# A two-layer hybrid decoder trunk: a new opening with the memory and x laid out features first

## The chip, the cores and the metric

The kernel runs on one core of a Trainium2 chip. The metric is the device time of one execution in microseconds (us), the median of several runs. The engines are TensorE (PE), VectorE (DVE), ScalarE (ACT), GpSimd (POOL) and SyncE (SP). SP and ACT issue the DMAs.

## The reference, cut to what matters

Two layers, each with 512 rows of 1024 features in x and 256 fixed memory tokens of 1024 features. Both x and the memory are normed over their features before a projection:

```python
def rmsnorm(x, g):
    return x * rsqrt(mean(x * x, axis=-1) + 1e-6) * g

def memory_read(q, mem_n, w_mem_kv):          # mem_n = rmsnorm(mem, mem_norm_g)
    k, v = split(mem_n @ w_mem_kv)            # 4 heads of 128 each
    p = softmax(q @ k.T * 128 ** -0.5)
    return p @ v

def hybrid_layer(x, mem, ...):
    proj = rmsnorm(x, pre_g) @ w_in           # 6664 columns, for four groups of heads
    y = concat(retention, ssd, stick_breaking, memory_read, each times its gate) @ w_out
    return x + rmsnorm(y, post_g)
```

The factor rsqrt(...) is a single number for each row of x or of the memory. It can be applied to a row before the projection, or to the row's results after it.

## The kernel before, in words

**Numbers in two parts.** Every operand of a product is split into a high part (fp32r, a cast on ACT) and a remainder (a subtraction on VectorE), and a product is made of three matmuls: high by high, high by low, low by high (`mm3`, `split`, `Pair`). "A product" below is one such matmul.

**Weights.** They come as blocks of 1 MB (128 x 2048), in the order in which they are used, on ACT's queue (`w_load`). Two such buffers exist (NRAW = 2), so that the load of block b+2 waits until both halves of block b have been split. Each half is a sub-block of 128x1024, split by ACT (`wh<-raw`) and VectorE (`wl<-raw,wh`) into one of five pairs of buffers (NSUB = 5, `w_prefetch`). Each layer's first two blocks hold the weights of the memory's keys, one sub-block for each head; the next two those of its values; then come those of x, beginning with the values of the stick-breaking heads (`sb_v`).

**Memory.** k0 to k3 are the keys of the four heads (`mem_k`, 24 products of 128x256 each, one sub-block); v0 and v1 are the values, two heads each (`mem_v`, two sub-blocks and 48 products each). Together they are 192 products. Keys and v go to TensorE's banks `pj`; four of these exist, and four `mx`.

**Norms.** `mem_norm` loads the memory with its rows on the partitions, squares and sums it on ACT, takes the power -0.5 on GpSimd, multiplies on VectorE by the deviation and the gain, transposes it on TensorE (`transposed`) and splits the result. x's four tiles of 128 rows (t = 0 to 3) go the same way in `prenorm`, into `hTh` and `hTl`. At the start the kernel does both, with the keys' products between x's tiles. For the second layer the memory is normed again, in the middle of the output projection (`out_proj`). x's tiles are normed at its end, as each row tile gets its post-norm (`post`), and the second layer's keys are made there too.

**Order.** Each engine takes its instructions from its own row, in order. In what order they stand there is decided by the framework's scheduler, which walks through the written program with times of its own. Buffers come from pools that go round; an instruction that needs a buffer waits for its last reader.

Of the kernel before, what the change touches and what calls it, by code (L numbers as in the profile page):

```python
# [15 lines left out]
DEPTH = 2  # L16
# [87 lines left out]
NPAR = 8 * 4 + 8 + 32 + 32 + 4 + 4 + 8  # L104
PO = dict(convw=0, convb=32, dtb=40, alog=72, dskip=104, ssdg=108, memg=112)


def pack_params(conv_w, conv_b, dt_bias, a_log, d_skip, ssd_norm_g, mem_norm_g):
    out = np.empty((P, DEPTH, NPAR), np.float32)
    for l in range(DEPTH):  # L110
        o = out[:, l]
        o[:, 0:32] = conv_w[l].reshape(4, 8, P).transpose(2, 1, 0).reshape(P, 32)
        o[:, 32:40] = conv_b[l].reshape(8, P).T
        o[:, 40:72] = np.repeat(dt_bias[l], 4)[None]
        o[:, 72:104] = np.repeat(a_log[l], 4)[None]
        o[:, 104:108] = np.repeat(d_skip[l], 64).reshape(4, P).T
        o[:, 108:112] = ssd_norm_g[l].reshape(4, P).T
        o[:, 112:120] = mem_norm_g[l].reshape(8, P).T
    return out

# [39 lines left out]
class Builder:  # L160
# [4 lines left out]
    def __init__(self, tc, pools, args, taps=None):  # L165
# [12 lines left out]
        self.nc.gpsimd.memset(self.eps4[:], EPS)  # L178

# [90 lines left out]
    def split(self, src, h, l, hf):  # L270
        self.nc.scalar.copy(h, src)  # L271
        self.nc.vector.tensor_sub(l, src, hf)  # L272
# [10 lines left out]
    def w_init(self):  # L283
        self.raw, self.sub = {}, {}
        self.nsubs = 2 * DEPTH * NBLK
        self.w_dma = self.w_off = self.w_split = self.w_cur = 0

    def w_prefetch(self):
        while self.w_split < min(self.nsubs, self.w_cur + self.NSUB):
# [5 lines left out]
            self.split(src, h, l, h.bitcast(F32))  # L295
            self.sub[k] = (h, l)
            self.w_split += 1
            if k % 2:
                del self.raw[k // 2]
                self.w_load(k // 2 + self.NRAW)  # L300

    def w_load(self, b):
        while self.w_dma <= min(b, DEPTH * NBLK - 1):
            n = block_width(self.w_dma)
            r = self.wp.tile([P, 2 * SUBD], F32, tag="raw", name=self.name("raw"), bufs=self.NRAW)
            src = self.a["wts"][self.w_off:self.w_off + P * n]
            self.nc.scalar.dma_start(r[:, :n], src.rearrange("(p n) -> p n", p=P))
# [21 lines left out]
    def proj_a(self, x=None, nt=NT, extra=0):  # L329
# [6 lines left out]
        banks = [self.mx() if t > 1 else self.pj() for t in range(nt // per)]  # L336
        for s in range(2):
# [8 lines left out]
            self.w_prefetch()  # L346
        return banks
# [43 lines left out]
    def load_rows(self, src, t):  # L391
        x = [self.buf(), self.buf()]
        for i in range(2):
            self.nc.sync.dma_start(x[i], src[P * t:P * t + P, 512 * i:512 * i + 512])
        return x

    def mem_norm(self, l):
        xs = [self.load_rows(self.a["mem"], t) for t in range(2)]
        gB = self.bcast_row(self.a["mem_norm_g"][l:l + 1])
        hns = [self.normed(x, gB) for x in xs]  # L400
        ps = [Pair(self) for _ in range(4)]

        for t in range(2):
            def out(k, b):
                for j in range(2):
                    p = ps[k // 2 + j]
                    s = slice(P * t, P * t + P)
                    self.split(v3(b[:, 256 * j:256 * j + 256], 2), v3(p.h, 2)[:, :, s], v3(p.l, 2)[:, :, s], v3(p.hf, 2)[:, :, s])
            self.transposed(hns[t], out)
# [5 lines left out]

    def mem_k(self, h):
        if h % 2 == 0:
            self.kT.append(Pair(self, 512, "y"))
        k, s = self.kT[h // 2], slice(N_MEM * (h % 2), N_MEM * (h % 2) + N_MEM)
        b = self.proj_b(self.mx_, N_MEM)  # L420
        self.split(b, k.h[:, s], k.l[:, s], k.hf[:, s])

    def mem_v(self):
        self.mv.append(self.pair(self.proj_a(self.mx_, 2)[0], "y"))
# [417 lines left out]
    def out_proj(self, l):  # L842
# [4 lines left out]
        for kc in range(16):  # L847
# [9 lines left out]
            if kc % 2:  # L857
                self.w_prefetch()
            if kc == 8 and not last:
                self.mem_norm(l + 1)  # L860
# [28 lines left out]
        if not last:  # L889
            for h in range(HEADS):  # L890
                self.mem_k(h)
# [26 lines left out]
    def build(self):  # L918
        nc = self.nc
        self.hTh, self.hTl = self.fixed(KC * SEQ, F32R, "hTh"), self.fixed(KC * SEQ, F32R, "hTl")  # L920
        self.hk = (lambda kc: self.hTh[:, SEQ * kc:SEQ * kc + SEQ], lambda kc: self.hTl[:, SEQ * kc:SEQ * kc + SEQ])
        self.w_init()
        nc.sync.dma_start(self.C[:, 0:P], self.a["consts"][:, 0:P])
        self.mem_norm(0)
        self.w_prefetch()
        preB = self.bcast_row(self.a["pre_norm_g"][0:1])
        self.xsrc = [self.a["x"][P * t:P * t + P] for t in range(NT)]
        for t in range(NT):
            self.prenorm(self.load_x(t), preB, t)
            self.mem_k(t)  # L930
        nc.sync.dma_start(self.C[:, P:NCON], self.a["consts"][:, P:NCON])
        nc.sync.dma_start(self.C[:, NCON:NCON + DEPTH * NPAR], self.a["params"])
        nc.vector.tensor_copy(self.b16[:, 0:P], self.con("ident", P))
        nc.vector.tensor_copy(self.b16[:, P:2 * P], self.con("neg", P))
        nc.vector.tensor_copy(self.onesr[:], self.con("ones", P))
# [4 lines left out]

    def layer(self, l):
        self.exp_ln_phase()
        for _ in range(2):
# [30 lines left out]
def lay_out(x, mem, pre_norm_g, post_norm_g, w_in, conv_w, conv_b, dt_bias, a_log, d_skip, ssd_norm_g, mem_norm_g,  # L974
# [3 lines left out]
        "mem": mem.reshape(N_MEM, D),  # L978
        "pre_norm_g": pre_norm_g,
        "post_norm_g": post_norm_g,  # L980
        "mem_norm_g": mem_norm_g,
        "wts": pack_weights(w_in, w_mem_kv, w_out),
        "params": pack_params(conv_w, conv_b, dt_bias, a_log, d_skip, ssd_norm_g, mem_norm_g).reshape(P, DEPTH * NPAR),
# [16 lines left out]
```

## Time and profile before

| | us |
|---|---|
| median of 3 runs | 982.67 |
| lowest and highest | 981.52, 983.36 |
| the profiled execution | 983.62 |
| its span from first to last instruction | 981.9 |
| TensorE busy | 956.9 |
| VectorE busy | 655.2 |
| ScalarE busy | 457.0 |
| GpSimd busy | 108.3 |

A row of the page or of a view has its time first, then its length, engine, line, operation, what it writes and reads (out<-in by the program's names), shapes and count; in brackets is how long the engine was idle before it and what ended that. All times are from the span's start. Products overlap in TensorE, so the distance between two starts is the price of one, not the length of its row. In a view of stretches each engine has its busy time and its count, in the order PE, PEld (weight loads), DVE, ACT, POOL, and then come the granted clock, the DMA engines' busy share and GB/s.

### The profile page before, as it was taken

How to read it: one execution, taken by the hardware profiler on the slowest of the kernel's cores; microseconds unless marked ns; L12 is line 12 of the kernel's file. 1: busy time of each engine (PE TensorE's matmuls, PEld its weight loads, DVE VectorE, ACT ScalarE, POOL GpSimd, SP SyncE). 2: the span in 40 equal slices, each digit the busy share in tenths (PEclk: the TensorE clock that was granted, in tenths of full speed). 3: DMA queues.
4: the chain of work that ended last, by engine and by line, in shares of the span. 5: the costliest groups of instructions: out<-in, count | busy, mean ns of one | idle time of the engine just before them, and what ended most of it. 6: DMA issues, size and time to landing. Idle time of an engine off the chain costs nothing.

```text
span 981.9 us, 13235 instructions
## 1 busy us (share of the span) xinstructions
PE 956.9 (97%) x5136; PEld 810.5 (83%) x5136; DVE 655.2 (67%) x1047; ACT 457.0 (47%) x848; POOL 108.3 (11%) x170
## 2 busy tenths in 40 slices
PE   3999999999999999999999999999999999999997
PEld 3998888988888788788899888898888878888885
DVE  5754566875867896766287455768776877867443
ACT  4733456633444443554265344765434543435341
POOL 1200000000242201020022000000002321102001
PEclk9999999999999999999999999999999999999999
DMA  9432211213142323264254321212123423323502
GB/s 356 156 130 86 84 46 44 86 49 123 44 144 102 119 91 126 74 204 155 102 195 151 130 86 44 86 44 86 49 84 93 140 97 118 113 91 119 191 24 85
DMA packets 26734, 106.84 MB, mean 109 GB/s; under 512 B 4144, under 2 KB 4528, under 8 KB 16944
## 3 DMA queue, kind: packets, MB, share of 16 engines
q10 hardware_dynamic: 10944, 79.76, 22.9%
q1 hardware_dynamic: 15728, 26.24, 8.3%
q8 instruction: 40, 0.66, 0.3%
q14 instruction: 22, 0.18, 0.1%
HBM read 101.68 MB, written 4.28 MB: 108 GB/s over the span
## 4 chain that ended last, share of the span: by engine, by line
PE 86%; DMA 5%; DVE 5%; ACT 1%; issue 1%; POOL 1%; DVEq 0%; SPq 0%; ACTq 0%; POOLq 0%
PE pj L263 63%; PE mx L263 20%; DMA s<-acs 1%; DMA r<-row 1%; DMA consts<-params 1%; DVE s L519 1%; PE mx L379 1%; DMA s<-mem 1%; DVE s L682 1%; PE mx L473 1%; DVE wl L272 1%; DMA t<-r 1%; POOL t L583 1%; DVE s L518 0%; DVE s L272 0%
## 5 line engine op out<-in xcount | busy, mean ns | idle before, releaser
L263 PE MATMUL pj<-hTh,wh 128*128 128x512 f32 x704 | 280.5, 398 | 0.0
L263 PE MATMUL pj<-hTl,wh 128*128 128x512 f32 x704 | 278.9, 396 | 0.0
L263 PE MATMUL pj<-hTh,wl 128*128 128x512 f32 x704 | 278.8, 396 | 0.0
L272 DVE TENSOR_TENSOR wl<-raw,wh 128x1024 fp32r<-128x1024 f32 (+1 forms) x152 | 185.7, 1224 | 126.2 <-ACT wh L271 119.8
L271 ACT CAST wh<-raw 128x1024 fp32r<-128x1024 f32 (+1 forms) x152 | 159.1, 1049 | 187.2 <-PE pj L263 155.6
L263 PEld LDWEIGHTS pj<-hTh,wl 128*128 128x128 f32 x704 | 132.3, 188 | 29.6 <-issue 0.2
L263 PEld LDWEIGHTS pj<-hTl,wh 128*128 128x128 f32 x704 | 132.4, 188 | 28.9
L263 PEld LDWEIGHTS pj<-hTh,wh 128*128 128x128 f32 x704 | 132.5, 188 | 28.3
L263 PE MATMUL pj<-wh,s 128*128 128x512 f32 (+1 forms) x384 | 105.0, 358 | 0.0
L263 PE MATMUL mx<-s,s 128*128 128x256 f32 (+4 forms) x616 | 97.6, 310 | 0.4 <-DVE s L272 0.4
L263 PEld LDWEIGHTS mx<-s,s 128*128 128x128 f32 (+1 forms) x616 | 84.5, 178 | 13.5 <-issue 3.2
L263 PE MATMUL mx<-wh,s 128*128 128x512 f32 x256 | 80.3, 393 | 0.0
L263 PEld LDWEIGHTS pj<-wh,s 128*128 128x128 f32 x384 | 68.0, 188 | 11.4
L263 PE MATMUL pj<-wl,s 128*128 128x512 f32 (+1 forms) x192 | 68.3, 356 | 0.0
L272 DVE TENSOR_TENSOR s<-mx,s 128x512 fp32r<-128x512 f32 (+2 forms) x100 | 47.1, 503 | 30.5 <-ACT s L271 30.3
L602 POOL TENSOR_SCALAR_AFFINE_SELECT s<-s 128x128 fp32r<-128x128 f32 x64 | 21.1, 362 | 417.6 <-DVE s L272 417.6
L263 PE MATMUL pj<-wh,hTh 128*128 128x256 f32 (+1 forms) x224 | 64.4, 287 | 0.4 <-DVE s L430 0.4
L271 ACT CAST s<-mx 128x512 fp32r<-128x512 f32 (+2 forms) x100 | 41.1, 446 | 49.2 <-PE mx L263 25.3
L263 PE MATMUL pj<-wl,hTh 128*128 128x256 f32 (+1 forms) x224 | 63.7, 284 | 0.0
L263 PE MATMUL pj<-wh,hTl 128*128 128x256 f32 (+1 forms) x224 | 62.9, 284 | 0.0
L263 PEld LDWEIGHTS mx<-wh,s 128*128 128x128 f32 x256 | 48.1, 188 | 10.9
L272 DVE TENSOR_TENSOR s<-y,s 128x512 fp32r<-128x512 f32 x64 | 41.3, 687 | 20.3 <-ACT s L271 14.5
(147 smaller groups left out, 1312.2 us busy)
## 6 DMA issues: line engine op xcount, KB each, us to landing
raw<-wts ACTq DMA_DIRECT2D x74, 1024.0 KB, 4.8
s<-x SPq DMA_DIRECT2D x24, 256.0 KB, 3.7
s<-acs SPq DMA_DIRECT2D x16, 256.0 KB, 6.6
r<-row SPq DMA_DIRECT2D x12, 256.0 KB, 3.7
raw<-wts ACTq DMA_DIRECT2D x2, 1056.0 KB, 5.2
s<-mem SPq DMA_DIRECT2D x8, 256.0 KB, 7.0
s<-acs SPq DMA_DIRECT2D x16, 128.0 KB, 5.5
x<-s SPq DMA_DIRECT2D x8, 256.0 KB, 2.3
```

Of the source, the lines that this page charges most:

```text
L263: return self.nc.tensor.matmul(out, lhsT, rhs, start=start, stop=stop)
L271: self.nc.scalar.copy(h, src)
L272: self.nc.vector.tensor_sub(l, src, hf)
L379: self.nc.tensor.transpose(b[:, P * j:P * j + P], hn[i][:, P * j:P * j + P], self.con("ident", P))
L473: nc.tensor.transpose(b[:, P * t:P * t + P], w[t // 2][:, o:o + P], self.con("ident", P))
L519: nc.vector.tensor_tensor_scan(out=u[:, ::-1], data0=u[:, ::-1], data1=u[:, ::-1], initial=0.0, op0=ALU.add, op1=ALU.bypass)
L583: nc.gpsimd.tensor_tensor(out=c, in0=c, in1=self.mhalf[:RP], op=ALU.pow)
L602: nc.gpsimd.affine_select(out=d, in_=d, pattern=[[1, P]], compare_op=ALU.is_ge, fill=0.0, base=0, channel_multiplier=-1)
L682: nc.vector.scalar_tensor_tensor(out=acc[:, s:], in0=b[:, :SEQ - s], scalar=tap(3 - s), in1=acc[:, s:], op0=ALU.mult, op1=ALU.add)
```

## The change

- **Layout.** The host passes x and the memory also with features on the partitions (`xT`, `memT`). Nothing is transposed on TensorE for the memory or for the first layer's x. Between the layers x is still normed and transposed as before.
- **Memory.** The raw memory times its gain is split (`mem_pairs`), and the keys and values are made of that. The deviation of each memory row comes from squares (ACT), additions (GpSimd), a product with a column of ones (`col_rstd`) and a power; `to_rows` spreads it as a row over all partitions by a product of ones with a diagonal matrix. Keys are multiplied by that row on VectorE before they are split (`mem_k2`), values by a column in their split (`mem_v`). The deviation is worked out once and used in both layers.
- **x of the first layer.** Its eight chunks of 128 features are squared, added up and normed in the same manner (`squares`, `col_rstd`, `to_rows`, `first_norm`); every second remainder is made on GpSimd.
- **Order.** The opening (`start`) is written by hand: its instructions enter their engines' rows in the order written. The scheduler takes over after it.
- **First work.** TensorE does 24 products of zeros (`warm_up`) while the first loads run. The first weight block is loaded and split in smaller pieces.
- The parameters get eight more columns (the gain of x's first norm).

The diff, cut to its core:

```diff
+    def warm_up(self):
+        self.nc.gpsimd.memset(self.b16[:], 0.0)
+        b = self.mx()
+        for _ in range(24):
+            self.mm(b[:, 0:2 * P], self.b16[:, 0:P], self.b16[:], True, True)
...
-    def proj_a(self, x=None, nt=NT, extra=0):
+    def proj_a(self, x=None, nt=NT, extra=0, mid=None):
...
             self.w_prefetch()
+            if s == 0 and callable(mid):
+                mid()
...
+    def mem_pairs(self, l, i):
+        nc, ps = self.nc, self.mp
+        for kc in (2 * i, 2 * i + 1):
+            p, s, g = ps[kc // 2], slice(256 * (kc % 2), 256 * (kc % 2) + 256), self.par(l, "memg", kc)
+            m = self.mraw[kc // 2][:, s]
+            nc.scalar.activation(p.h[:, s], m, AF.Copy, scale=g)
+            nc.vector.scalar_tensor_tensor(out=p.l[:, s], in0=m, scalar=g, in1=p.hf[:, s], op0=ALU.mult, op1=ALU.subtract)
+
+    def squares(self, raws, acc=None):
+        nc = self.nc
+        for x in raws:
+            q = self.buf()
+            nc.scalar.activation(q, x, AF.Square, scale=1.0 / 32.0)
+            if acc is None:
+                acc = q
+            else:
+                nc.gpsimd.tensor_tensor(out=acc, in0=acc, in1=q, op=ALU.add)
+        return acc
+
+    def col_rstd(self, sq, n, r):
+        b = self.mx()
+        for t in range(n):
+            self.mm(b[:, t:t + 1], sq[:, P * t:P * t + P], self.con("ones", 1), True, True)
+        self.nc.vector.tensor_scalar(out=r, in0=b[:, :n], scalar1=EPS, scalar2=None, op0=ALU.add)
+        self.nc.gpsimd.tensor_tensor(out=r, in0=r, in1=self.mhalf[:, :n], op=ALU.pow)
+
+    def to_rows(self, r, n):
+        d = self.buf(P * n)
+        for t in range(n):
+            self.nc.vector.tensor_scalar(out=d[:, P * t:P * t + P], in0=self.con("ident", P), scalar1=r[:, t:t + 1],
+                                         scalar2=None, op0=ALU.mult)
+        b = self.mx()[:, :P * n]
+        self.mm(b, self.con("ones", P), d, True, True)
+        return b
...
-        b = self.proj_b(self.mx_, N_MEM)
-        self.split(b, k.h[:, s], k.l[:, s], k.hf[:, s])
+        t = self.buf(N_MEM)
+        self.nc.vector.tensor_tensor(out=t, in0=b, in1=self.mrow[:], op=ALU.mult)
+        self.split(t, k.h[:, s], k.l[:, s], k.hf[:, s])
...
+    def first_norm(self, xs, rows, first):
+        H, HF, L = self.hTh[:], self.hTh[:].bitcast(F32), self.hTl[:]
+        for kc, x in enumerate(xs, first):
+            s = slice(SEQ * kc, SEQ * kc + SEQ)
+            self.nc.vector.scalar_tensor_tensor(out=x, in0=x, scalar=self.par(0, "preg", kc), in1=rows, op0=ALU.mult, op1=ALU.mult)
+            self.nc.scalar.copy(H[:, s], x)
+            (self.nc.gpsimd if kc % 2 else self.nc.vector).tensor_tensor(out=L[:, s], in0=x, in1=HF[:, s], op=ALU.subtract)
...
+            if kc == 6 and not last:
+                self.mem_load(nc.sync, range(4))
             if kc == 8 and not last:
-                self.mem_norm(l + 1)
+                self.mem_tiles()
+                for i in range(4):
+                    self.mem_pairs(l + 1, i)
...
             for h in range(HEADS):
-                self.mem_k(h)
+                self.mem_k2(h, self.mem_k(h))
...
+    def start(self):
+        nc = self.nc
+        self.warm_up()
+        nc.sync.dma_start(self.C[:, NCON:NCON + DEPTH * NPAR], self.a["params"])
+        self.mem_load(nc.sync, (0, 1))
+        self.w_load(1)
+        nc.sync.dma_start(self.C[:, 0:4 * P], self.a["consts"][:, 0:4 * P])
+        self.mem_tiles()
+        self.mem_pairs(0, 0)
+        self.w_prefetch(1)
+        for i in range(1, 4):
+            self.mem_pairs(0, i)
+        k = [self.mem_k(0)]
+        self.w_prefetch(2)
+        xT = [self.buf() for _ in range(KC)]
+        for kc in range(KC):
+            i = nc.sync.dma_start(xT[kc], self.a["xT"][:, SEQ * kc:SEQ * kc + SEQ])
...
+        q = self.squares([self.mraw[i] for i in range(2)])
+        k.append(self.mem_k(1))
+        self.w_prefetch(3)
+        q = self.squares([self.mraw[i] for i in range(2, 4)], q)
+        nc.gpsimd.tensor_tensor(out=q[:, :N_MEM], in0=q[:, :N_MEM], in1=q[:, N_MEM:], op=ALU.add)
+        self.w_prefetch(4)
+        k.append(self.mem_k(2))
+        self.col_rstd(q, 2, self.mcol[:])
+        k.append(self.mem_k(3))
+        self.w_prefetch(5)
+        q = self.squares(xT[:2])
+        nc.scalar.copy(self.mrow[:], self.to_rows(self.mcol, 2))
+        for h in range(2):
+            self.mem_k2(h, k[h])
+        self.w_prefetch(6)
+        q = self.squares(xT[2:5], q)
+        for h in range(2, HEADS):
+            self.mem_k2(h, k[h])
+        q = self.squares(xT[5:], q)
+        r = self.tiny(NT)
+        self.w_prefetch(7)
+        self.mem_v(lambda: self.col_rstd(q, NT, r))
+        self.w_prefetch(8)
+        rows = self.to_rows(r, NT)
+        self.first_norm(xT[:4], rows, 0)
+        self.w_prefetch(9)
+        self.mem_v(True)
+        self.first_norm(xT[4:], rows, 4)
```

98 lines of the change are left out of this document (53 added, 45 removed).

## The prediction

> **What bounds the kernel now.** I read the page first, then TensorE's waits, the chain that ended last, and counts of products by stretch.
>
> ```profile
> span 981.9 us, 13235 instructions
> PE 956.9 (97%) x5136; PEld 810.5 (83%) x5136; DVE 655.2 (67%) x1047; ACT 457.0 (47%) x848; POOL 108.3 (11%) x170
> PE   3999999999999999999999999999999999999997
> PE mx L379 <- DVE s L371: 15.1, 2, 14.9
> PE mx L263 <- DVE r L619: 1.8, 2, 0.9
> ```
>
> TensorE is busy for 97% of the span. Only the first slice is low, and of its waits one is long: 14.9 us for the first transposes; the next group has 1.8 in all. So the time is a start, then TensorE's own list of work. A change gains by starting that list earlier or shortening it, and loses wherever it makes TensorE wait.
>
> The chain of waits shows the start:
>
> ```profile
> 1.23 7.99 DMA s<-mem
> 9.24 9.46 DMA consts<-params
> 19.97 14.46 PE pj L263 x108
> 34.43 0.44 PE mx L379 x4
> ```
>
> The first product starts at 19.97 us; four transposes take 0.44, so one is 0.11. Next, TensorE's products in four stretches (after the range: length, then busy time and count; TensorE comes first):
>
> ```profile
> 19.97:23.70 3.73, 3.73 (x17) 3.73 (x18) 3.34 (x8) 3.14 (x8) 0.14 (x1) 1.00 1.05 402
> 23.70:27.43 3.73, 3.73 (x34) 3.73 (x33) 0.00 (x1) 0.00 (x0) 0.09 (x1) 1.00 0.66 248
> 511.50:524.50 13.00, 13.00 (x113) 13.00 (x113) 13.00 (x19) 9.98 (x20) 3.82 (x6) 1.00 0.50 166
> 14.94 1.97 PE L379 MATMUL mx<-consts,s 128*128 128x128 f32 x8 [14.94 <-DVE s L371]
> ```
>
> Between 511.5 and 524.5 us a 128x256 product takes 13.00/113 = 0.115. The first 3.73 us hold 17 products, the next 34: TensorE begins at half speed, though the granted clock reads 1.00 in both, and that costs 3.73/2 = about 1.9. The last row shows eight transposes in 1.97 after the idle start, also slow; they did not end the half speed.
>
> To compare starts I use one mark: the moment by which all 192 products of the memory and all of x's transposes would be done if TensorE did nothing else. Before, that is 19.97 + 192 x 0.115 (22.1) + 32 x 0.11 (3.5) + 1.9 = **47.4**. The changed kernel has no transposes of x; its mark is when TensorE can take x's first products.
>
> **The new start.** The prices, by group, busy us and mean ns:
>
> ```profile
> L272 DVE TENSOR_TENSOR wl<-raw,wh 128x1024 fp32r<-128x1024 f32 x12 | 14.5, 1222 | 11.6 <-ACT wh L271 11.6
> L271 ACT CAST wh<-raw 128x1024 fp32r<-128x1024 f32 x13 | 13.4, 1046 | 12.3 <-PE pj L263 4.7 <-DMA raw<-wts 4.7 <-PE mx L263 2.9
> L371 DVE SCALAR_TENSOR_TENSOR s<-s,t,s 128x512 f32<-128x512 f32 x12 | 8.5, 749 | 3.0 <-POOL t L357 3.0
> L366 ACT ACTIVATE s<-s 128x512 f32<-128x512 f32 x12 | 7.5, 627 | 1.5 <-DMA s<-mem 1.1 <-DMA s<-x 0.4
> L272 DVE TENSOR_TENSOR hTl<-mx,hTh 128x512 fp32r<-128x512 f32 x8 | 5.3, 684 | 0.0
> L272 DVE TENSOR_TENSOR y<-pj,y 128x256 fp32r<-128x256 f32 x4 | 1.6, 418 | 0.0
> L271 ACT CAST y<-pj 128x256 fp32r<-128x256 f32 x4 | 1.4, 372 | 0.0
> L934 DVE CAST b<-consts 128x128 bf16<-128x128 f32 x1 | 0.2, 220 | 0.0
> L729 POOL TENSOR_SCALAR_AFFINE_SELECT s<-s 128x512 f32<-128x512 f32 x16 | 13.8, 871 | 20.8 <-DVE s L728 18.5 <-ACT s L731 1.3 <-issue 1.0
> 6.12 1.99 ACT L271 CAST wh<-raw 128x1024 fp32r<-128x1024 f32 x2 [3.13 <-DMA raw<-wts]
> ```
>
> First product: the last row has the first 1 MB of weights in at 6.12. Now half of it suffices, beside params and a first part of the memory, so between 5 and 6.1. Two memory casts (2 x 0.37), a half cast and a half subtraction (about 0.55 and 0.65) follow: **7.6**, 12.4 earlier than before. The products on zeros run before it and cost nothing, as nothing else is there to do.
>
> From there k0 to k3 and v0's first half are 120 products, 13.8 us. The memory's column sums and its row product are small f32 products: between 0.12 and 0.45 each by the rows above, together 0.9. Feeding costs waits: ACT has by k3's weights 8 x 0.37 + 4 x 1.05 + 4 x 0.63 = 9.7 us to do from 5.5 on, then a subtraction of 1.22, so k3 can't start before 16.5; waits of 1 to 4 in all, I take 2.5. End of v0's first half: **24.8**.
>
> There TensorE needs the sum of x's squares (col_rstd stands in the middle of v0), and this is where the change loses. ACT's row, first before, then changed (y is k's pair, raw the next weight block, s_339 to s_362 x's squares):
>
> ```order
> 23 L366 ACTIVATE s46_197,t45_196<-s43_192 128x512
> 24 L271 CAST wh54_248<-raw33_172 128x1024
> 25 L271 CAST y51_221<-pj53_223 128x256
> 26 L366 ACTIVATE s47_198,t45_196<-s44_193 128x512
> 27 L271 CAST wh66_310<-raw38_182 128x1024
> 28 L271 CAST y51_221<-pj65_285 128x256
> ```
>
> Now six squares of x stand behind the DMA issue of block 4, which waits until VectorE has split block 2:
>
> ```order
> 24 L1041 COPY mrow_81<-mx52_322 128x256
> 25 L284 CAST y18_156<-s53_325 128x256
> 26 L284 CAST y18_156<-s54_329 128x256
> 27 L284 CAST wh55_333<-raw23_187 128x1024
> 28 L326 DMA raw57_337<-wts 128x2112
> 29 L441 ACTIVATE s58_339<-s26_191 128x512
> 30 L441 ACTIVATE s59_342<-s27_192 128x512
> 31 L441 ACTIVATE s60_345<-s28_193 128x512
> 32 L284 CAST y42_253<-s61_348 128x256
> 33 L284 CAST y42_253<-s62_352 128x256
> 34 L441 ACTIVATE s63_356<-s29_194 128x512
> ```
>
> Two more squares follow row 34. That a row waits for the one ahead is seen before:
>
> ```profile
> 28.17 1.05 ACT L271 CAST wh<-raw 128x1024 fp32r<-128x1024 f32 x1 [4.69 <-PE pj L263]
> 29.39 0.63 ACT L366 ACTIVATE s<-s 128x512 f32<-128x512 f32 x1
> 26.00:28.00 2.00, 2.00 (x20) 2.00 (x20) 0.00 (x0) 0.00 (x0) 0.00 (x0) 1.00 0.11 43
> ```
>
> ACT idled 4.69 us at the cast (row 24) though x, the last load of that phase, was in (DMA share 0.11 from 26 us), and squared only behind it.
>
> The walk: row product done at 22.0; mrow 22.5; VectorE multiplies by mrow (0.42), y cast, subtraction and next multiplication, y cast: 24.7; cast of weights 25.7; subtraction 27.0; DMA issue 27.4; three squares 29.3; two casts with their VectorE steps 31.0; three squares **32.9**. GpSimd adds each square to the sum. No row has a 128x512 addition of two inputs there; bounds are 0.87 (the one-input select) and twice that. I take 1.2, nearer to the row. The chain of adds then ends at **35.3**: TensorE is idle for 10.5. The Trainium skill, page "GPSIMD Engine Reference", section "3.1 Elementwise — side-by-side cycle accounting", gives 4497 ns for an addition of 2048 elements, by an estimate of a quarter 1.12; by it the sum would be 0.4 lower, and no row before tests it.
>
> After 10.5 idle I count half speed again, as after the idle start: four small sums and 24 products end at 40.3. Then v0's two scalings (0.74), cast, subtraction (stands ahead on VectorE), four diagonal multiplications at 0.22 and hand-overs: 44.5, so 4.0 idle. Row product 0.8, 48 products 5.5, and half speed again between 0 and 1.9, I take 1.0: 51.8. Meanwhile VectorE makes x's first four chunks (4 x 0.75 + 2 x 0.69, two waits for ACT): 50.9; only then stands the split of the next weights, 2.3, and a hand-over: mark **54.0**, or **+6.6**. Chunks 4 to 7 are hidden behind x's products with the first half of two weight blocks (96 products, 11 us).
>
> On the half speed: the rows show it after 15 us of idleness and never after under 1. The Trainium skill, page "TensorE: Matmul & The Clock Gate", Part 1, says the clock falls back after an idle window of about 3.4 us, which speaks against every new wait here; by it the 4.0 costs a full 1.9 and the sum is 0.9 higher.
>
> **The layer boundary.** The second memory pass loses 16 transposes, **-1.8**. But k now goes through a multiplication by mrow on VectorE before TensorE's bank comes free, and v0 needs the first of these banks. VectorE before, and the changed kernel's (y906 the second pair of k, L371 and L394 the normed t=2, L475 the multiplications by mrow):
>
> ```order
> 523 L272 TENSOR_TENSOR wl909_4842<-raw851_4530,wh908_4841 128x1024
> 524 L272 TENSOR_TENSOR y906_4815<-pj907_4816,y905_4814 128x256
> 525 L272 TENSOR_TENSOR y906_4815<-pj911_4849,y905_4814 128x256
> 526 L272 TENSOR_TENSOR wl913_4875<-raw901_4779,wh912_4874 128x1056
> 527 L272 TENSOR_TENSOR hTl_80<-mx874_4634,hTh_79 128x4x128
> 528 L905 TENSOR_TENSOR s886_4711<-mx799_4295,s785_4265 128x512
> 529 L371 SCALAR_TENSOR_TENSOR s881_4676<-s828_4412,t883_4681,s786_4268 128x512
> ```
>
> In the changed kernel the reads of the banks have moved from ahead of t=2 to behind it:
>
> ```order
> 514 L394 SCALAR_TENSOR_TENSOR s851_4611<-s798_4347,t853_4616,s756_4203 128x512
> 515 L394 SCALAR_TENSOR_TENSOR s852_4612<-s799_4348,t853_4616,s757_4204 128x512
> 516 L980 SCALAR_TENSOR_TENSOR s800_4351<-s761_4210,t858_4649,s800_4351 128x512
> 517 L980 SCALAR_TENSOR_TENSOR s801_4352<-s856_4646,t858_4649,s801_4352 128x512
> 518 L285 TENSOR_TENSOR hTl_80<-mx854_4621,hTh_79 128x4x128
> 519 L475 TENSOR_TENSOR s872_4716<-pj868_4685,mrow_81 128x256
> 520 L475 TENSOR_TENSOR s876_4749<-pj873_4720,mrow_81 128x256
> ```
>
> TensorE's row now, from the end of k3 on (pj884 k3, L402 transposes of t=1 and t=2, pj888 v0); before, v0 followed k3 at once and filled the time:
>
> ```order
> 2595 L276 MATMUL pj884_4790<-s726_4045,wl820_4462 128x256
> 2596 L402 MATMUL mx844_4569<-consts_72,s841_4559 128x128 x4
> 2597 L402 MATMUL mx845_4576<-consts_72,s842_4560 128x128 x4
> 2598 L402 MATMUL mx854_4621<-consts_72,s851_4611 128x128 x4
> 2599 L402 MATMUL mx855_4628<-consts_72,s852_4612 128x128 x4
> 2600 L276 MATMUL pj888_4824<-wh834_4532,s720_4039 128x256
> ```
>
> When that is, on before's clock:
>
> ```profile
> 511.33 0.28 PE L263 MATMUL pj<-s,wl 128*128 128x256 f32 x1
> 511.44 0.28 PE L263 MATMUL pj<-wh,s 128*128 128x256 f32 x1
> 514.76 0.75 DVE L272 TENSOR_TENSOR y<-pj,y 128x256 fp32r<-128x256 f32 x2
> 517.79 1.41 DVE L371 SCALAR_TENSOR_TENSOR s<-s,t,s 128x512 f32<-128x512 f32 x2
> ```
>
> k3 ends and v0 begins at 511.4. VectorE is full from 511.5 to 524.5 (13.00 above). Without the four y subtractions (1.4) t=2 is normed from 517.79 - 1.4 = 516.4 on. TensorE: t=1's transposes end at 512.3, t=2's halves run at 517.1 and 517.8; then VectorE's two of L980, hTl and the first L475 end at 520.1, so v0 starts at 520.2. Idle 520.2 - 511.4 - 1.8 of transposes = **7.0**, and half speed after it, 1.9 (transposes did not end it at the start): **+8.9**.
>
> The rest of the second pass I cost at nothing. SP issues the memory's four loads earlier, ahead of the last row of deviations:
>
> ```profile
> 419.37 1.00 SPq L394 DMA_DIRECT2D s<-mem  x2
> 423.79 0.33 SPq L587 DMA_DIRECT2D r<-row  x1
> 427.75 1.42 DVE L818 SCALAR_TENSOR_TENSOR y<-y,consts,r 128x512 f32<-128x512 f32 x2 [5.04 <-DMA r<-row]
> 453.33 2.77 DVE L866 TENSOR_TENSOR s<-pj,s 128x512 f32<-128x512 f32 x4 [1.17 <-PE pj L263]
> ```
>
> Four issues are some 2 us, so y comes at about 430 instead of 428; its products are the last of the half that ends at 453, some 20 us later. Without that cover each us late would count in full. The casts of the memory on ACT and VectorE take the place of its squares, normed rows and splits, behind the same products.
>
> Sum: 6.6 - 1.8 + 8.9 = 13.7. The profiled execution took 983.62; that gives 997.3. The median, 982.67, stands 0.95 under it: **996.4**. The rest of the list only shifts: TensorE's work there is the same.
>
> **Rivals.**
> - Boundary covered (VectorE reaches L475 by 512): 8.9 goes, 987.5. Against it: the fixed order and a full VectorE. 0.08.
> - x's sum ready by 25: 10.5, its half speed 1.9 and the 1.0 go, about 983; within 0.2% (2 us, about what a measurement tells). 0.04.
> - Faster: the waits do not hold the queues, that is, ACT and VectorE reach the later rows while the earlier wait. Both places vanish: mark 24.8 + 0.5 + 2.8 + 0.8 + 5.5 + 0.8 = 35.2, 12.2 under before's 47.4, with -1.8 is 968.7. It decides from x's sum being done by 25 and L475 by 512. The 4.69 row speaks against. 0.07.
> - GpSimd's adds dear. Under a busy VectorE a small operation took ten times its usual time:
>
> ```profile
> 522.97 2.28 POOL L351 TENSOR_SCALAR t<-t 128x1 f32<-128x1 f32 x1 [4.80 <-ACT s L366]
> 23.56 0.22 POOL L351 TENSOR_SCALAR t<-t 128x1 f32<-128x1 f32 x1 [7.32 <-ACT s L366]
> ```
>
> At 2.3 per add, six from 28.0 end at 41.8, 6.5 later: 1003. 0.08.
> - The zeros do nothing: k0 at half speed, +1.9, 998. Inside the forecast.
>
> Forecast 0.73. Faster 0.07, same 0.04, slower 0.89. The range leaves out the cases under 986 (0.11): 986 to 1003.
>
> **Right or wrong.** Right if TensorE's waits show one of 9 to 12 us at about 25 for GpSimd's sum, one near 40 for the diagonal, and 4 to 6 near the boundary for the normed t=2, then products of half rate. Wrong if first x-products start before 47, or if v0 of the second layer follows k3 within 2 us.

## The result and the profile after

| | before | after |
|---|---|---|
| median, us | 982.19 (4 runs) | 1010.01 (4 runs) |
| lowest and highest | 981.52, 983.36 | 1009.66, 1011.76 |
| the profiled execution | 983.62 | 1009.8 |
| its span | 981.9 | 1008.0 |

The ratio is 1.0285, with an interval of 1.0268 to 1.0303: 27.8 us slower, where 13.7 were forecast. Two executions, one of e6_scheduler below (3401.80 us) and one of the kernel before beside e12_paced_chunks (1056.26 us), lie far off all others and are left out of the times. The page of the changed kernel, its span, TensorE's busy time, and TensorE's rows of busy time and of granted clock in forty slices:

```profile
span 1008.0 us, 13162 instructions
PE 967.6 (96%) x5112; PEld 816.0 (81%) x5112; DVE 657.6 (65%) x1056; ACT 457.3 (45%) x834; POOL 116.7 (12%) x164
PE   7489999999999999999997999999999999999997
PEclk9689999999999999999998999999999999999999
```

The low first slice has become three (7, 4, 8), and a new one stands in the middle (a 7, at the layer boundary). The clock is below 1.00 in both places. TensorE's list of waits:

```profile
PE mx L276 <- POOL s L445: 12.2, 1, 12.2
PE mx L402 <- DVE s L394: 6.0, 1, 6.0
PE mx L276 <- DVE s L460: 5.3, 2, 4.7
PE pj L276 <- ACT wh L284: 2.3, 2, 2.0
```

The first three are the waits that the prediction named: GpSimd's sum of x's squares, the normed tile t=2 at the boundary, and the diagonal. To see how much each place took, two marks late in the program serve, which do the same work in both kernels: GpSimd's first masking of a stick-breaking head, and a reciprocal of the second layer. Before:

```profile
227.49 1.80 POOL L602 TENSOR_SCALAR_AFFINE_SELECT s<-s 128x128 fp32r<-128x128 f32 x7 [181.29 <-DVE s L272]
600.34 0.17 DVE L458 RECIPROCAL t<-t 128x2 f32<-128x2 f32 x1
```

After:

```profile
244.31 1.77 POOL L671 TENSOR_SCALAR_AFFINE_SELECT s<-s 128x128 fp32r<-128x128 f32 x7 [163.56 <-DVE s L285]
625.45 0.17 DVE L527 RECIPROCAL t<-t 128x2 f32<-128x2 f32 x1
```

The opening cost 244.31 - 227.49 = **16.8** (forecast 6.6), the boundary 625.45 - 600.34 - 16.8 = **8.3** (forecast 8.9 - 1.8 = 7.1). The last 1.0 of the span's 26.1 came later. So the boundary was sized well and the opening was not.

The opening by the chain of work that ended last (start, length, engine, what):

```profile
21.00 0.62 PE mx L276 x4
...
30.95 0.64 ACT s L441
...
39.53 1.27 POOL s L445
40.84 7.21 PE mx L276 x32
...
51.74 0.88 DVE s L460 x4
52.75 2.06 PE mx L276 x2
...
61.49 0.98 ACT wh L284
62.50 1.48 DVE wl L285
64.02 2.94 PE pj L276 x22
```

Read downwards it is the walk of the prediction: memory's sums (21.00), x's squares (30.95), GpSimd's additions to 40.8, x's column sums and 24 products, diagonal and row product, x's chunks, then the split of x's first weights. TensorE takes up x's products for good at 64.02, against the forecast mark of 54.0.

The granted clock in stretches of 3.4 us (range, length, busy time and count of each engine, then clock, DMA share, GB/s):

```profile
7.45:10.86 3.41, 3.41 (x14) 3.18 (x15) 3.41 (x8) 3.28 (x8) 0.00 (x0) 0.50 1.05 432
41.60:45.00 3.40, 3.40 (x17) 3.40 (x17) 0.16 (x1) 0.00 (x0) 1.04 (x1) 0.50 0.00 0
48.45:51.86 3.41, 0.00 (x0) 0.00 (x0) 2.23 (x4) 1.56 (x3) 0.00 (x0) 0.99 0.00 0
55.27:58.65 3.38, 3.38 (x18) 3.38 (x17) 2.32 (x4) 1.58 (x3) 0.30 (x1) 0.50 0.24 95
```

The clock was half for k0's first products, in spite of the zeros. It was half again from 31.3 us to 48.4, came back just as TensorE had run out of work, fell at 51.8 and was half until 58.65. All of TensorE's work between 40.8 and 58.6 ran at half rate.

At the boundary, by the timeline of each engine, TensorE's transposes and v0's first product, and VectorE's multiplications that free the bank:

```profile
526.77 1.04 PE L402 MATMUL mx<-consts,s 128*128 128x128 f32 x8
533.83 1.94 PE L402 MATMUL mx<-consts,s 128*128 128x128 f32 x8 [6.02 <-DVE s L394]
536.75 0.55 PE L276 MATMUL pj<-wh,s 128*128 128x256 f32 x1 [0.98 <-ACT hTh L284]
...
536.19 1.07 DVE L475 TENSOR_TENSOR s<-pj,mrow 128x256 f32<-128x256 f32 x3
```

v0 comes 0.56 us after the first L475 starts: 6.02 + 0.98 = 7.0 idle, the forecast to the tenth. (The name beside the second wait is the one that came last by the profile; by the order of the rows v0 also needs the bank that L475 frees.)

### The profile page after: what moved, and what is told of

It reads as the page before. It is cut to its first block, busy times and chain, and to the rows that moved or that the text cites. A ratio compares the mean times of both kernels' runs of the same rounds, so it can differ in the third digit from the quotient of the medians.

```text
span 1008.0 us, 13162 instructions
## 1 busy us (share of the span) xinstructions
PE 967.6 (96%) x5112; PEld 816.0 (81%) x5112; DVE 657.6 (65%) x1056; ACT 457.3 (45%) x834; POOL 116.7 (12%) x164
## 4 chain that ended last, share of the span: by engine, by line
PE 81%; DVE 7%; DMA 4%; ACT 3%; POOL 2%; issue 2%; SPq 0%; DVEq 0%; ACTq 0%; POOLq 0%
PE pj L276 59%; PE mx L276 21%; DVE wl L285 1%; DMA r<-row 1%; DMA s<-acs 1%; POOL s L445 1%; DVE s L588 1%; DVE s L751 1%; PE mx L542 1%; DMA s<-memT 1%; DMA t<-r 1%; POOL t L652 1%; ACT wh L284 1%; DVE s L587 0%; PE mx L602 0%
## 5 line engine op out<-in xcount | busy, mean ns | idle before, releaser
L285 DVE TENSOR_TENSOR wl<-raw,wh 128x1024 fp32r<-128x1024 f32 (+2 forms) x153 | 186.8, 1224 | 133.4 <-ACT wh L284 125.8
L284 ACT CAST wh<-raw 128x1024 fp32r<-128x1024 f32 (+2 forms) x153 | 159.0, 1042 | 182.4 <-PE pj L276 153.8
L276 PE MATMUL mx<-wh,s 128*128 128x512 f32 (+1 forms) x320 | 97.2, 387 | 0.0
L276 PE MATMUL pj<-wh,s 128*128 128x512 f32 (+1 forms) x320 | 93.3, 375 | 1.0 <-ACT hTh L284 1.0
L276 PEld LDWEIGHTS mx<-wh,s 128*128 128x128 f32 x320 | 61.6, 201 | 11.6 <-issue 0.5
L276 PEld LDWEIGHTS pj<-wh,s 128*128 128x128 f32 x320 | 59.1, 192 | 12.8 <-ACT hTh L284 1.4
L276 PE MATMUL mx<-wl,s 128*128 128x512 f32 (+1 forms) x160 | 60.9, 382 | 0.0
L276 PE MATMUL pj<-wl,s 128*128 128x512 f32 (+1 forms) x160 | 59.9, 374 | 0.0
L285 DVE TENSOR_TENSOR s<-mx,s 128x512 fp32r<-128x512 f32 (+2 forms) x84 | 41.0, 517 | 28.3 <-ACT s L284 28.1
L285 DVE TENSOR_TENSOR s<-y,s 128x512 fp32r<-128x512 f32 x64 | 41.2, 686 | 20.4 <-ACT s L284 14.5
```

The lines of the kernel that those rows point to most:

```text
L276: return self.nc.tensor.matmul(out, lhsT, rhs, start=start, stop=stop)
L285: return self.nc.vector.tensor_sub(l, src, hf)
```

## The experiments

The theory: the operations fit, but the rows of ACT and VectorE hold the ones TensorE waits for behind others that nobody waits for, at three places of the opening and one of the boundary; each wait then brings half-rate work. The rivals: the chain of operations behind x's deviation is long in any order; GpSimd's additions alone are at fault; loads or VectorE's total work hold the opening.

Medians and ratios to the kernel before, measured beside each group. The medians of before ran from 982.46 to 983.76 over the groups, so that differences below some 2 us are read from the profiles.

| run | us | ratio, interval | under 1010.0 |
|---|---|---|---|
| e1_boundary | 1000.18 | 1.0163 (1.0146 to 1.0180) | 9.8 |
| e2_vector_adds | 1007.88 | 1.0243 (1.0228 to 1.0258) | 2.1 |
| e3_early_squares | 1003.19 | 1.0194 (1.0175 to 1.0213) | 6.8 |
| e4_filler | 1008.07 | 1.0245 (1.0227 to 1.0262) | 1.9 |
| e5_early_diag | 1007.86 | 1.0260 (1.0243 to 1.0277) | 2.2 |
| e6_scheduler | 1000.51 | 1.0180 (1.0154 to 1.0205) | 9.5 |
| e7_no_zeros | 1009.73 | 1.0275 (1.0257 to 1.0292) | 0.3 |
| e8_mended_start | 998.37 | 1.0162 (1.0143 to 1.0180) | 11.6 |
| e9_mended_both | 989.66 | 1.0074 (1.0058 to 1.0090) | 20.4 |
| e10_sum_first | 992.63 | 1.0099 (1.0079 to 1.0119) | 17.4 |
| e11_memory_adds | 1008.59 | 1.0264 (1.0242 to 1.0286) | 1.4 |
| e12_paced_chunks | 986.79 | 1.0038 (1.0026 to 1.0050) | 23.2 |

**The boundary alone.**

```diff
 def mem_pairs(self, l, i):
             m = self.mraw[kc // 2][:, s]
+            if l:
+                nc.gpsimd.tensor_tensor(out=m, in0=m, in1=self.mrow[:], op=ALU.mult)
...
 def mem_k2(self, h, b):
+        t = b
+        if self.starting:
+            t = self.buf(N_MEM)
+            self.nc.vector.tensor_tensor(out=t, in0=b, in1=self.mrow[:], op=ALU.mult)
...
 def mem_v(self, mid=None):
+        if not self.starting:
+            self.mv.append(self.pair(self.proj_a(self.mx_, 2)[0], "y"))
+            return
```

> Second layer only: GpSimd multiplies the raw memory by the row of deviations during the first layer's output projection (8 multiplications of 128x256, some 0.7 us each), so its keys and values are split straight from TensorE's banks, as in the kernel before. Theory (the keys' multiplication stands behind the normed t=2 and t=3 on VectorE and holds the bank): the waits of 6.0 and 1.0 us at 533 us and the half-rate products behind them go; 1010.0 falls by 10 to 11, to 999 to 1000. Rival (VectorE is full there anyway, the wait only moves to the next reader): under 4 us, 1006 or more. Second rival (the eight multiplications hold up the second pass of the memory): no change or slower.

Measured 9.8 lower. TensorE's two longest waits now, the 6.0 gone; and by the timeline GpSimd's eight multiplications and the second mark:

```profile
PE mx L276 <- POOL s L447: 12.2, 1, 12.2
PE mx L276 <- DVE s L462: 4.7, 1, 4.7
```

```profile
437.24 5.63 POOL L434 TENSOR_TENSOR s<-s,mrow 128x256 f32<-128x256 f32 x8
617.07 0.17 DVE L534 RECIPROCAL t<-t 128x2 f32<-128x2 f32 x1
```

The mark came 8.4 earlier than in the changed kernel (625.45), and 9.7 earlier when counted from the first mark, which came 1.4 later in this execution (245.67). GpSimd's 5.63 us stood where it had nothing else to do. The wait was the multiplication's place in VectorE's row, as the theory has it.

**The price or the place of the additions.** Two runs, one for each half of the question.

```diff
-                nc.gpsimd.tensor_tensor(out=acc, in0=acc, in1=q, op=ALU.add)
+                (nc.gpsimd if mem else nc.vector).tensor_tensor(out=acc, in0=acc, in1=q, op=ALU.add)
```

> The seven additions of x's squares go from GpSimd (1.3 to 2.1 us each) to VectorE (0.69); everything else stays. Theory (the sum is late by GpSimd's price): the sum is ready at about 36.5 instead of 40.8 us, TensorE's wait falls from 12.2 to about 8, total 3.5 to 4.5 lower: 1005.5 to 1006.5. Rival (the sum is late because ACT's squares stand behind the casts, and VectorE's row is held by them): within 1.5 us of 1010.

```diff
-        q = self.squares(xT[:2])
+        q = self.squares(xT)
         nc.scalar.copy(self.mrow[:], self.to_rows(self.mcol, 2))
...
-        q = self.squares(xT[2:5], q)
...
-        q = self.squares(xT[5:], q)
```

> All eight squares of x stand right behind the first two in ACT's row, ahead of mrow and the keys' casts; additions stay on GpSimd. Theory (the place in ACT's row makes the sum late): x is in by 24.3, squares end near 27, GpSimd's chain near 34 to 36 instead of 40.8; the keys come 1 to 2 us later, which only the bank waits could see; total 5 to 7 lower, 1003 to 1005. Rival (GpSimd's seven additions alone set it: 22 + 7 x 2.1 = 37 or later): 2 to 4 lower. Second rival (the delay of the keys and weights takes it back): within 1.5 us of 1010.

With cheap additions on VectorE the wait for the sum was still 10.3 us; by VectorE's timeline three additions waited there for the squares, which still stood late in ACT's row:

```profile
PE mx L276 <- DVE s L445: 10.3, 1, 10.3
```

```profile
32.77 2.28 DVE L445 TENSOR_TENSOR s<-s,s 128x512 f32<-128x512 f32 x3 [1.07 <-ACT s L441]
```

That is 2.1 lower in the time and 0.7 in the first mark (243.6), between the two expectations. With early squares and GpSimd's dear additions it was 6.8 lower; the wait is 5.4, and by the timeline GpSimd's seven additions now run without a pause:

```profile
PE mx L276 <- POOL s L445: 5.4, 1, 5.4
```

```profile
23.38 10.52 POOL L445 TENSOR_TENSOR s<-s,s 128x512 f32<-128x512 f32 x7
```

So the place in ACT's row came first. Once it is mended, GpSimd's price (10.52 / 7 = 1.50 each) is what holds the sum, until 33.9.

**The clock.** Products on zeros fill the waits.

```diff
-        for _ in range(24):
+        for _ in range(42):
...
-    def col_rstd(self, sq, n, r):
+    def col_rstd(self, sq, n, r, fill=0):
...
         b = self.mx()
+        self.zeros(fill, b)
...
-        self.mem_v(lambda: self.col_rstd(q, NT, r))
+        self.mem_v(lambda: self.col_rstd(q, NT, r, 112))
...
-        rows = self.to_rows(r, NT)
+        rows = self.to_rows(r, NT, 40)
```

> Products on zeros fill TensorE's waits: 42 instead of 24 at the start, 112 ahead of x's column sums, 40 ahead of x's row product. Nothing is waited for less. Theory (after each long wait the granted clock is 0.5, and it costs 1.7 at the start, 3.5 around the sums and 3 to 4 around the row product): clock 1.00 from 8 to 62 us, total 6 to 9 lower, 1001 to 1004. Rival (other engines set the times in the opening, TensorE's rate is hidden): within 2 us of 1010. Second rival (zeros do not count as work for the clock): 0.5 as before, no change.

Three stretches, with TensorE's busy time first and the clock third from the end:

```profile
22.70:26.10 3.40, 3.40 (x17) 3.39 (x16) 2.33 (x3) 0.69 (x2) 1.28 (x1) 0.51 0.97 358
26.10:40.80 14.70, 14.70 (x133) 13.43 (x132) 6.20 (x10) 7.02 (x13) 7.98 (x6) 1.00 0.31 115
40.80:57.00 16.20, 15.90 (x129) 14.15 (x127) 7.40 (x14) 3.75 (x6) 3.08 (x3) 1.00 0.19 66
```

Zeros do hold the clock: it was 1.00 from 26 to 57 us. Before that it was half for one stretch, from 22.7 us, behind a wait of 1.4. Yet the run was only 1.9 lower, at the bound of the first rival: TensorE was done with v1 at 57.0 instead of 62.2 and then waited for the same chunks and the same weight split. Half rate cost about 2 us here and not 6 to 9; the rest lay beside VectorE's work.

> The 24 products on zeros are left out. Theory (the clock was granted half again from 7.45 to 10.9 us, since the zeros end at 5.4 and the first product comes at 7.43): nothing is lost, within 1 us of 1010. Rival (zeros make the first products faster after all, or the first product is due earlier without them): 1.5 to 2 either way.

Without the first zeros, 1009.73: no change. With them, they ended at 5.4 and the first product came at 7.43; k0's products ran at half rate in both runs, without the zeros up to 12.9 us and with them up to 10.9.

**The diagonal.**

```diff
-        self.mem_v(lambda: self.col_rstd(q, NT, r))
+        d = []
+        self.mem_v(lambda: (self.col_rstd(q, NT, r), d.append(self.diag(r, NT))))
...
-        rows = self.to_rows(r, NT)
+        rows = self.to_rows(d[0], NT)
```

> The four diagonal multiplications of x's deviation stand on VectorE ahead of v0's two scalings and a weight split instead of behind them; nothing else moves. Theory (the 4.7 us wait for the row product is a matter of VectorE's row): the diagonal is done at about 45 us, the row product follows v0's second half at 48.1 instead of 52.75; x's first chunks then wait for VectorE's scalings and weight split (to 51.8 instead of 54.8), so 3 us lower, 1006 to 1008. Rival (TensorE's own time counts in full, and its clock stays at 1.00 behind it): 6 to 8 lower, 1002 to 1004. Second rival (the split of x's first weights, which stands behind x's chunks, sets the end in any case): under 1.5.

2.2 lower, within the theory's range. The 4.7 at the row product is gone, and a wait of 4.55 has come up where x's first products stand:

```profile
59.05 0.81 PE L276 MATMUL pj<-wh,hTh 128*128 128x264 f32 x2 [4.55 <-ACT wh L284]
```

These start at 59.05 instead of 62.5; the wait went from the diagonal to the weight split behind x's chunks.

**Memory's additions.** Its four additions go to VectorE in the same manner.

> The four additions of the memory's squares go from GpSimd to VectorE; x's stay. Theory (GpSimd's 2.1 us an addition makes the memory's row 1.4 late, and the later rows with it): the wait of 1.4 for that sum goes, mrow at 24.0 to 24.5 instead of 25.84, x's squares and all behind them as much earlier, total 1 to 2 lower, 1008 to 1009. Rival (the additions hold VectorE's weight splits, which hold TensorE): 0 to 2 slower.

ACT's timeline where mrow is copied:

```profile
24.31 0.38 ACT L1041 COPY mrow<-mx 128x256 f32<-128x256 f32 x1 [2.42 <-PE mx L276]
```

mrow was copied at 24.31 instead of 25.84, the first mark came 1.5 earlier (242.8), and the run was 1.4 lower, as the theory has it.

**The order as a whole.** The scheduler orders the opening.

```diff
-        with self.tc.manual_schedule():
-            self.start()
+        self.start()
```

> The opening is put in order by the scheduler that orders the rest, instead of standing as written; the operations are the same. Theory (the written order, not the operations, makes TensorE wait): x's squares go ahead of the keys' casts, the wait for x's sum falls below 6 us, total 4 to 12 lower. Rival (the chain of operations behind x's sum is long in itself: 8 squares, 7 additions, sums, power, diagonal, row): within 3 us of 1010. Second rival (the scheduler's own times mislead it here): slower by 3 or more.

TensorE's waits, and the first mark in GpSimd's timeline:

```profile
PE mx L402 <- DVE s L394: 7.2, 1, 7.2
...
PE mx L276 <- POOL s L445: 3.8, 1, 3.8
```

```profile
233.66 2.03 POOL L671 TENSOR_SCALAR_AFFINE_SELECT s<-s 128x128 fp32r<-128x128 f32 x8 [173.74 <-DVE s L285]
```

9.5 lower with the same operations: the sum's wait fell from 12.2 to 3.8, and the first mark came at 233.66, so 10.6 of the opening's 16.8 are gone. The written order, not the operations, made most of its loss. But only part of it was the order that the theory names. The squares do go ahead of the keys' casts, yet x's sum came only 1.8 us earlier (39.02 instead of 40.84), since GpSimd's six additions took 9.45 us. The rest of the shorter wait is other work: TensorE was busy until 35.2 us instead of 28.6, with all of v0, 24 more products, ahead of the column sums. And x's first products (53.58 instead of 62.52) found their weights split, since ACT's casts of them stand ahead of x's chunks (31.89 instead of 61.40). The boundary's wait is still there, 7.2.

**All moves together.** The diff of the opening, cut to its core; the column sums take both lists of squares into one bank:

```diff
+        qs = [self.squares(xT[:4]), self.squares(xT[4:], eng=nc.vector)]
...
+        self.mem_v(lambda: (self.col_rstd(qs, NT, r), d.append(self.diag(r, NT))))
...
+        rows = self.to_rows(d[0], NT)
+        self.w_prefetch(9)
         self.first_norm(xT[:4], rows, 0)
-        self.w_prefetch(9)
```

> Four moves in the opening, none in the second layer: x's eight squares right behind the first two; three additions on GpSimd and three on VectorE, in two chains that TensorE's column sums join; the diagonal ahead of v0's scalings; the first split of x's weights ahead of x's norm. Theory (the four waits are all of the start's loss): x's sum at 28 to 30 us, so no wait over 2 us there, row product at 33 to 35, x's first products at 41 to 44 instead of 62.5 to 64, total 19 to 22 lower, 988 to 991. Rival (weights' loads and splits come next and hold the start at 50 or later): 10 to 14 lower, 996 to 1000.

> The mended start, the second layer's memory multiplied by the deviations on GpSimd beforehand, and 42 products on zeros instead of 24. Theory (waits at the start 20, boundary 11, first clock 1.5): 30 to 34 under 1010, 976 to 980, so under the kernel before by 0.3 to 0.8%. Rival (a second limit in the opening, loads or splits): 984 to 990, no faster than before.

The mended start gave 11.6 and not 19 to 22, both mends together 20.4 and not 30 to 34: the times are those of the rivals. In the first run nothing waited for x's sum any more, but x's first products came at 49.38, not at 41 to 44. What held the start there is only in part what the rivals name: in the second run's chain of work the load of a weight block takes 4.69 us (from 44.75), but ahead of it TensorE's two row products waited for VectorE:

```profile
29.30 1.22 PE L276 MATMUL mx<-s,consts 128*128 128x256 f32 x2 [4.63 <-DVE s L462]
...
41.76 1.10 PE L276 MATMUL mx<-s,consts 128*128 128x512 f32 x2 [2.35 <-DVE s L462]
```

The memory's diagonal now stood behind x's additions on VectorE, and x's diagonal behind four keys. The next run moved both ahead, and the keys behind x's norm.

```diff
+        dm = self.diag(self.mcol, 2)
+        qs = [self.squares(xT[:4]), self.squares(xT[4:], eng=nc.vector)]
+        self.w_prefetch(6)
+        nc.scalar.copy(self.mrow[:], self.to_rows(dm, 2))
...
+            self.col_rstd(qs, NT, r)
+            d.append(self.diag(r, NT))
+            self.w_prefetch(8)
...
+        self.first_norm(xT[:4], rows, 0)
+        for h in range(2):
+            self.mem_k2(h, k[h])
+        self.w_prefetch(10)
+        self.mem_v(True)
+        self.first_norm(xT[4:], rows, 4)
```

> As the run with both mended, with 36 products on zeros, and with VectorE's row in another order: the memory's diagonal ahead of the additions of x's squares; x's sum, power and diagonal ahead of all four keys' multiplications; two keys behind x's first norm, two at the end of the opening; two more weight splits ahead. Theory (in that run VectorE's row, not TensorE, set the start: 4.6 and 2.4 us of waits for its diagonals, and a start of x at 48.6): memory's row product at 24 to 25 us, x's at 32 to 34, x's first products at 41 to 43, total 5 to 7 lower than the 989.7 of that run, 982 to 985, about as fast as the kernel before. Rival (VectorE's total work in the opening sets it, whatever its order): x's first products at 47 or later and 987 to 990. Second rival (keys made late hold TensorE's banks): slower than 990.

x's first product came at 41.8, as the theory had it, and the run was still some 2 to 3 us slower than the one before it. That is the time of the second rival, though TensorE's waits show none for a bank that a late key held; the longest is for x:

```profile
PE pj L276 <- ACT hTh L502: 6.1, 1, 6.1
```

x's fifth chunk had fallen behind in VectorE's row, where two keys, three weight splits and v1's two scalings stand ahead of it, and TensorE worked at half rate meanwhile. The last run paces the chunks.

```diff
 def first_norm(self, xs, rows, first):
...
+        def low(kc, x, s):
+            (self.nc.gpsimd if kc % 2 else self.nc.vector).tensor_tensor(out=L[:, s], in0=x, in1=HF[:, s], op=ALU.subtract)
...
             self.nc.scalar.copy(H[:, s], x)
+            late.append((kc, x, s))
+            if len(late) > 1:
+                low(*late.pop(0))
+        low(*late.pop(0))
...
+        self.first_norm(xT[4:], rows, 4)
+        self.mem_v(True)
```

> As the run with x's sum first, with two changes in VectorE's row: in x's norm each remainder stands one chunk later, so that VectorE scales the next chunk while ACT casts; and the second four chunks stand ahead of v1's scalings and two keys. Theory (there VectorE's order paced TensorE: 6.1 us of wait for the fifth chunk and half-rate products from 44.5 to 65): that wait falls below 2 us, the clock stays at 1.00, total 5 to 9 lower than the 992.6 of that run, 983 to 988, not under the kernel before. Rival (VectorE's total work, not its order, holds the opening): 989 or more. Second rival (with the waits gone the new opening beats the old): under 980.

TensorE's waits, the opening's last 17 us by stretch, and the first mark:

```profile
PE pj L276 <- DVE hTl L501: 2.7, 1, 2.7
...
PE pj L276 <- ACT hTh L505: 1.8, 1, 1.8
```

```profile
41.00:58.00 17.00, 12.05 (x75) 11.24 (x76) 15.45 (x20) 10.32 (x16) 5.36 (x4) 0.84 0.33 124
```

```profile
229.74 2.01 POOL L687 TENSOR_SCALAR_AFFINE_SELECT s<-s 128x128 fp32r<-128x128 f32 x8 [171.24 <-DVE s L285]
```

986.79, in the expected 983 to 988, and 23.2 under the changed kernel. The wait for the fifth chunk fell from 6.1 to 1.8, with 2.7 for a remainder; but the clock did not stay at 1.00 (0.84 between 41 and 58 us). VectorE is busy for 15.45 of those 17 us, so its total work may hold the opening now. That is not shown: no run gave it less to do there, and its order still counts, as the chain that ended last has two weight splits ahead of the remainder that TensorE waited for:

```profile
49.84 3.34 DVE wl L285 x2
53.18 0.61 DVE hTl L501
```

The first mark is at 229.74, still 2.3 behind the kernel before. No version tried here beats that kernel; this one comes closest, 0.26 to 0.50% above it.

## Why the prediction was right in its mechanism and wrong in its size

- **Right: the three waits and their names.** x's sum (forecast 9 to 12, measured 12.2), the diagonal, t=2 at the boundary (forecast 4 to 6, measured 6.0). The first x products came at 62.5, not before 47. The first two waits stood later than forecast: the one for the sum began at 28.6 instead of about 25, the one for the diagonal at 48.0 instead of near 40.
- **Right: the boundary.** Idle 7.0 against 7.0; that it agrees to the tenth is luck, since the forecast's parts were some 4.8 before t=2's transposes and 2.2 behind their start, and 6.0 and 1.0 were measured. Half rate behind it took 0.9 in the transposes and, with 16 products between 536.75 and 540.15 at 0.21 instead of 0.115, some 1.6 in v0: 2.5 against 1.9. The run that undid this part confirms 9.8 in the time. The 16 transposes gave back 1.5 of the forecast 1.8, by the marks of that run: it is 18.2 behind the kernel before at the first (245.67 - 227.49) and 16.7 at the second (617.07 - 600.34).

```profile
245.67 1.53 POOL L678 TENSOR_SCALAR_AFFINE_SELECT s<-s 128x128 fp32r<-128x128 f32 x6 [164.50 <-DVE s L285]
```

- **Wrong in size: the mark of the opening, 54.0 forecast and 64.0 measured.** This is the failed term, 10.0 of the 12.4 us by which the spans' difference of 26.1 is over 13.7. By the steps of its walk:

| step | forecast | measured | more |
|---|---|---|---|
| x's sum ready | 35.3 | 40.8 | 5.5 |
| sums and 24 products after it | 5.0 | 7.2 | 2.2 |
| wait for the diagonal (from there to the row product; 44.5 - 40.3, which the prediction writes as 4.0 idle) | 4.2 | 4.7 | 0.5 |
| row product, until x's first chunk | 0.8 | 2.1 | 1.3 |
| four chunks | 5.6 | 6.7 | 1.1 |
| split of x's weights | 3.1 | 2.5 | -0.6 |

- **x's sum.** "Row product done at 22.0" came at 25.8, since two of the memory's own additions cost 2.1 us each and its power 1.6; the squares ended at 35.7 instead of 32.9; and the additions behind them took 1.3 to 2.1, not 1.2. The first of these was not in the sum at all: feeding costs were counted for casts and subtractions, and the memory's additions on GpSimd were left out. The run with the memory's additions moved gave 1.5 of it back.
- **Half rate.** It was entered as 1.9 after one idle time and as 1.0 after the other. In the trace one low stretch ran from 31.3 to 48.4, and the next began 3.4 us later, so that the column sums (1.86), the 24 products, the row product (2.06) and half of v1 all ran at half rate. The step "row product 0.8" failed by this: it is 1.10 at the full clock (the rows of the run with both mended) and 2.06 here. The filler run shows, however, that this counted for about 2 us in the time and not for the 5.2 by which TensorE was done with v1 earlier, since VectorE's chunks and splits came next.
- **The range.** Its upper end of 1003 was the case of additions at 2.3 us each, every other step being as forecast. The errors of the steps had the same sign, and the range took in only one of them. The rival "the zeros do nothing" came true beside the forecast, and cost the time nothing: in the filler run, where k0 went at full rate, the last product of k0 to k2 began at 19.31 us, and here at 19.32.
- **The faster rival** (waits do not hold the queues) fell: moving squares ahead of the casts moved the sum by 6.9 us, so the rows do hold their later instructions back.

## What to carry to other kernels

When a product, a column sum or a row is put between two stretches of TensorE's work, look for the last instruction that it needs in the row of each helping engine, and count everything ahead of it there, the DMA issues and what they wait for as well. In the walk through several engines here five of six steps were too short: price every step, and let the range hold errors of one sign in all of them. And after one wait is mended look again at who is last: here six moves that promised 30 to 34 us together gave 20, and in that run TensorE waited 7.0 us for two diagonals in VectorE's row.

## What the runs showed of the hardware

- **An addition on GpSimd and VectorE's subtraction slow each other.** GpSimd's additions of 128x512, first one beside which VectorE works only in the last 0.4 us, then two beside VectorE, and VectorE's weight subtraction, first alone, then beside them:

```profile
14.39 1.29 POOL L445 TENSOR_TENSOR s<-s,s 128x512 f32<-128x512 f32 x1 [13.21 <-ACT s L441]
15.93 4.21 POOL L445 TENSOR_TENSOR s<-s,s 128x512 f32<-128x512 f32 x2 [0.24 <-ACT s L441]
```

```profile
11.49 1.23 DVE L285 TENSOR_TENSOR wl<-raw,wh 128x1024 fp32r<-128x1024 f32 x1 [0.42 <-ACT wh L284]
...
17.27 1.73 DVE L285 TENSOR_TENSOR wl<-raw,wh 128x1024 fp32r<-128x1024 f32 x1 [0.50 <-ACT wh L284]
```

 1.29 became 2.1 (4.21 / 2), and 1.23 became 1.73. With VectorE idle throughout, the addition took 1.27 (the row at 39.53 above). The Trainium skill, page "GPSIMD Engine Reference", section "8. Key points", says that GpSimd shares its interfaces to the on-chip memory with VectorE, with contention for VectorE's instructions that have two such inputs; the trace agrees, and the subtraction has two. The 1.12 that was worked out from that page's table is below even the undisturbed 1.27.

- **The clock changes on a fixed grid.** The changes at 7.45, 10.86, 31.34, 48.41, 51.82, 58.65, 533.10 and 539.92 us (read from the clock of stretches of 0.2 us) lie a whole number of 3.413 us apart; from the first to the sixth, 51.20 us, it is 15. The Trainium skill, page "TensorE: Matmul & The Clock Gate", Part 1, says that a free-running window of 3413 ns decides; the trace agrees. What wasn't expected: a stretch in which TensorE showed work throughout (41.6 to 45.0, its first microsecond the column sums with one result column each) did not bring the clock back. In the filler run the clock was lost at 22.7, behind a window (19.28 to 22.69) with a wait of 1.4 us and two such sums; TensorE was busy for 2.02 us of it. In the changed kernel the same wait lies in a window (17.69 to 21.10) with 2.01 us busy but hardly any of the sums, and the clock stayed at 1.00. That suggests that such sums count for little; how much work a window must hold, no run here measures.

- **Ahead of its first change the granted clock reads 1.00 at half rate too.** In the run without zeros k0's products start 0.21 us apart from 8.61 to 12.88 us and 0.11 apart from 13.03 on, with a granted clock of 1.00 throughout. So the half speed that the prediction read from the pace of the kernel before, at 1.00, was real.
